# Retention samples: keys of each sample in a zero-padded matrix of 128 rows, and one sine table instead of two

## The chip, the cores and the metric

One core of a Trainium2 chip runs the whole program. The metric is device time in microseconds, as the median of several executions. Engines are named as in the profile: PE is TensorE (PEld its weight loads), DVE VectorE, ACT ScalarE, POOL GpSimd, SP SyncE, which issues the weight transfers.

## The reference, cut to what matters

One inference step of a two-layer decoder trunk for two groups of requests that share all weights: a prompt of 256 positions from zero state, and 8 samples of one position each from carried states. Layer 0 mixes with RWKV-7 and S5, layer 1 with retention, and a SwiGLU block follows each. Retention has 8 heads, with 256 query and key entries and 512 value entries each. For every sample and head the new state, a matrix of 256 x 512, is the old one times a decay plus an outer product, and the output is the query times the new state:

```
q = rotary(p[..., :D_MODEL]...);  k = rotary(...) * DK ** -0.5
S = S * chunk_decay + einsum('bjhd,bjhe->bhde', k, v)     # j = 1 for a sample
o = q S                                                  # what q reads of the new state
rotary(x): concatenate([x1 * cos - x2 * sin, x2 * cos + x1 * sin])
```

## The kernel before

Activations lie transposed: features on the 128 partitions, 264 columns (256 prompt positions, then 8 samples). All large weights stream through once. A *granule* is 4 blocks of 128x128 weights: SP loads them, ACT rounds them to the high part `wh`, DVE subtracts for the low part `wl`, and TensorE does three matmuls of 264 columns per block (`xh,wh`, `xh,wl`, `xl,wh`), 12 per granule. There are four buffers of each part, and `split_to` (line 467) runs two granules ahead of TensorE (`LS = 2`).

Everything else is *side work*: Python generators that record operations, which a planner places between the stream's matmuls. `pump` (line 516) is called twice per granule. It keeps a model clock for each engine, and emits a recorded operation when its operands are there by that clock; side matmuls are emitted only if `ready <= now`, with `now` the model clock of TensorE, and up to a budget. `cost` (line 213) holds the model's durations, `after` (line 240) its waits. It sees overlaps in cells of 16 columns (`GRAIN`), so neighbours that share a cell count as dependent. The order so planned is the order of each engine's queue on the chip, and each engine works its queue strictly in order; a waiting instruction holds up all that is behind it.

Buffers come from named areas. `hold` (line 359) takes a whole area (`hidx`, `hidy`, `hida`, `hidb`, `tmp`), `arenas` and `cut` (lines 417 and 422) slice small tiles from a list of areas, first fit. Layer 0 cuts its scratch from all five areas, `hidx` first; layer 1 cuts from `hidy` and `tmp` (`TMPN` = 14990 columns) and takes `hidx` (1056 columns) for the keys and values `kvr` of the samples.

In layer 1, `ret_mix(h)` (line 1475) does the prompt's part of head h, and `ret_sample(h)` (line 1555) the samples'. For each of the heads, `ret_sample`

- loads the states of samples 0 to 3, 512 KB each, through POOL's queue into `S`;
- spreads keys and values of the samples, split into a high and a low part, over zeroed matrices `kc` and `vc`, so that after a transpose the 8 rows 32b to 32b+7 hold sample 4g+b (high and low combinations, whose products add up);
- transposes the keys of all 8 samples (4 transposes into one PSUM bank) and copies them with one ACT instruction to `kr` (128x512); the same for the values, `vr`;
- for each group g of four samples and each sample b: two outer products with 8 rows and 512 columns, one for each half d of the keys, and behind each a DVE instruction that scales the old state and adds the product; then the store of the state:

```
rows = slice(32 * b, 32 * b + 8)
P.matmul(p, kr[rows, (2 * g + d) * 128:(2 * g + d + 1) * 128], vr[rows], start=True, stop=True)
self.stt(r["S"][b][:, d], r["S"][b][:, d], gam, p, OP.mult, OP.add)
```

- then multiplies the queries with the four states (8 matmuls with 32 output rows each), and after g = 0 loads the states of samples 4 to 7.

The rotation in `ret_mix` multiplies the two halves, swapped, with a table `ssin` that holds -sin and sin beside each other (528 columns; POOL), multiplies with `cos` in place and adds (DVE). The tables are loaded at the start of layer 1 by `ret_setup` (line 1441), which also clears `qm`, `kc` and `vc` on POOL.

Of the kernel before, what the change touches and what calls it, by code (L numbers as in the profile page):

```python
# [10 lines left out]
F32R = mybir.dt.float32r  # L11
I32 = mybir.dt.int32
AF = mybir.ActivationFunctionType
OP = mybir.AluOpType
# [6 lines left out]
T = TP + TS  # L21
# [11 lines left out]
HID = FFN_PARTS[1]  # L33
HIX = FFN_PARTS[0] - HID
RH, DK, DV = 8, 256, 512
TMPN = 14990
NSET = 2
MOST = 3.3, 2.6
GRAIN = 16
# [84 lines left out]
def bc(ap, shape):  # L124
    return ap.to_broadcast(shape)


class Builder:
# [287 lines left out]

    def arenas(self, names):

        size = {"hida": HID * T, "hidb": HID * T, "hidx": HIX * T, "hidy": HIX * T, "tmp": TMPN}
        self.ar = [[self.hold(n, [128, size[n]], F32, "ar_" + n), 0, size[n], n] for n in names]  # L420

    def cut(self, *shape, parts=128):
# [248 lines left out]
    def ffn_tasks(self, i):  # L671
        I = self.I
        wg, wu, wd = I["ffn_w_gate"][i], I["ffn_w_up"][i], I["ffn_w_down"][i]
        tasks = []
        st = {}
        sp = self.t1[:, KT * T:].rearrange("p (a t) -> p a t", a=8)
        f0 = 0
        for part, nf in enumerate(FFN_PARTS):
            def gate(acc, f):
                if f == 0 or f == FFN_PARTS[0]:  # L680
                    st["h"] = [self.hold("hida", [128, HID, T], F32R, "hh")]
                    st["l"] = [self.hold("hidb", [128, HID, T], F32R, "hl")]
                    if f == 0:
                        st["h"].append(self.hold("hidx", [128, HIX, T], F32R, "hhx"))
                        st["l"].append(self.hold("hidy", [128, HIX, T], F32R, "hly"))
                s = sp[:, f % 3]
                self.mul(s, acc[:, :T], self.rstd)
                self.act(s, s, AF.Silu)
                st[f] = s

            def up(acc, f, fl):
                u = sp[:, 3 + f % 2]
                self.mul(u, acc[:, :T], self.rstd)
                self.mul(u, u, st.pop(f))
                self.split(*rh(fl), u)

            def down(acc, k, part):
                if part and k == KT - 4:
                    self.functions(ACT_SET[AF.Ln])
                self.add(self.x[:, k], self.x[:, k], acc[:, :T])  # L700
                if part == len(FFN_PARTS) - 1:
                    self.x_final(i, k)

            rx = self.rx
            rh = lambda k: (st["h"][k // HID][:, k % HID], st["l"][k // HID][:, k % HID])
            for f in range(f0, f0 + nf, 2):
                for e in range(2):
                    tasks.append(Task(wg, 0, KT, (f + e) * 128, rx, lambda a, f=f + e: gate(a, f)))
                for e in range(2):
                    tasks.append(Task(wu, 0, KT, (f + e) * 128, rx, lambda a, f=f + e, fl=f + e - f0: up(a, f, fl)))  # L710
            for k in range(KT):
                tasks.append(Task(wd, f0, nf, k * 128, rh, lambda a, k=k, part=part: down(a, k, part)))
            f0 += nf
        return tasks
# [726 lines left out]
    def ret_setup(self):  # L1441
        self.arenas(["hidy", "tmp"])
        c = self.cut
        self.kvr = self.hold("hidx", [128, HIX * T], F32R, "kvr")
        self.omh = self.hold("hida", [128, HID, T], F32R, "omh")
        self.oml = self.hold("hidb", [128, HID, T], F32R, "oml")
        sp = self.t1[:, KT * T:]
        r = self.rm = dict(q=[c(2, T), c(2, T)], k=[c(2, T), c(2, T)], v=c(4, T), g=[c(4, T), c(4, T)], B=c(2, T), mask=c(TP),
                           att=c(TP + 128), vt=c(2, 512), kt=c(2, 256), S=[c(2, 512) for _ in range(4)],
                           kc=c(2, 2, 128), vc=c(4, 128), qm=c(2, TS, 32), st=c(2, 512),  # L1450
                           o=sp[:, :4 * T].rearrange("p (a t) -> p a t", a=4),
                           sq=sp[:, 4 * T:].rearrange("p (a t) -> p a t", a=4))
        o, n = CONST_AT["cos"][0], self.C0.shape[1]
        late = c(n - o)
        self.QS.dma_start(late, self.C0[:, o:])
        for name in ("cos", "ssin", "dist"):
            at, w = CONST_AT[name]
            self.k[name] = late[:, at - o:at - o + w]
        for n in ("qm", "kc", "vc"):
            self.G.memset(r[n], 0.0)  # L1460

    def ret_in(self, acc, n, h, i):
        r = self.rm
# [11 lines left out]
    def ret_mix(self, h):  # L1475
        r, k, P = self.rm, self.k, self.P
        B, o, sq = r["B"], r["o"], r["sq"]
        for n in "qk":
            yield from self.wait((n, h))
            x = r[n][h % 2]  # L1480
            self.tt(B, x[:, ::-1], k["ssin"].rearrange("p (a t) -> p a t", a=2), OP.mult, self.G)
            self.mul(x, x, bc(k["cos"][:, None, :], [128, 2, T]))
            self.add(x, x, B)
            yield
        self.flags.add(("rot", h))
        q, kk = r["q"][h % 2], r["k"][h % 2]
# [2 lines left out]
        p = self.psum()  # L1489
# [65 lines left out]
    def ret_sample(self, h):  # L1555

        r, k, P = self.rm, self.k, self.P
        yield from self.wait(("rs", h - 1))
        src, dst = self.I["state_ret"], self.O[7]

        def load(g):
            for b in range(4):
                self.QG.dma_start(r["S"][b], src[h, 4 * g + b])

        load(0)
        yield from self.wait(("rot", h), ("v", h))
        v, kk = r["v"][:, :, TP:], r["k"][h % 2][:, :, TP:]
        qm = r["qm"].rearrange("p a b c -> p a (b c)")[:, :, 0:7 * 33 + 1:33]
        self.gcopy(qm, r["q"][h % 2][:, :, TP:])

        for g in range(2):
            for x, to, hi, lo in ((kk, r["kc"][:, g], slice(0, 3, 2), slice(1, 4, 2)), (v, r["vc"], slice(0, 2), slice(2, 4))):
                n = to.shape[1]
                at = to.rearrange("p a (j w) -> p a j w", j=4)[:, :, :, 4 * g:4 * g + 4]
                x4 = bc(x[:, :, 4 * g:4 * g + 4, None], [128, n, 4, 2])
                self.act(at[:, :, :, hi].bitcast(F32R), x4, AF.Copy)
                self.tt(at[:, :, :, lo].bitcast(F32R), x4, at[:, :, :, hi], OP.subtract)
        self.flags.add(("kv", h))
        yield
        kr, vr = self.kvr[:, :512], self.kvr[:, 512:1024]  # L1580
        p = self.psum()
        for i in range(4):
            P.transpose(p[:, i * 128:(i + 1) * 128], r["kc"][:, i // 2, i % 2], self.ident)
        self.act(kr, p, AF.Copy)
        p = self.psum()
        for e in range(4):
            P.transpose(p[:, e * 128:(e + 1) * 128], r["vc"][:, e], self.ident)
        self.act(vr, p, AF.Copy)
        yield
        yield from self.wait(("ret", h - 1))  # L1590
        gam = math.exp(LOGG[h])
        po = self.banks[4]
        for g in range(2):
            for b in range(4):
                rows = slice(32 * b, 32 * b + 8)
                for d in range(2):
                    p = self.psum()
                    P.matmul(p, kr[rows, (2 * g + d) * 128:(2 * g + d + 1) * 128], vr[rows], start=True, stop=True)
                    self.stt(r["S"][b][:, d], r["S"][b][:, d], gam, p, OP.mult, OP.add)
                self.QG.dma_start(dst[h, 4 * g + b], r["S"][b])  # L1600
                yield
            for d in range(2):
                for b in range(4):
                    P.matmul(po[32 * b:32 * b + 32], r["qm"][:, d, 4 * g + b], r["S"][b][:, d],
                             start=g == 0 and d == 0, stop=g == 1 and d == 1, tile_position=(0, 32 * b))
            if g == 0:
                load(1)
            yield
        osb = self.flat(r["sq"])[:, :512]
        self.act(osb, po, AF.Copy)  # L1610
        yield
        p = self.psum()
        for e in range(4):
            P.matmul(p[:, 8 * e:8 * e + 8], osb[:, e * 128:(e + 1) * 128], k["sel"], start=True, stop=True)
        self.V.tensor_copy(r["o"][:, :, TP:], p[:, :32].rearrange("p (e b) -> p e b", e=4))
        self.flags.add(("rs", h))
        yield
# [71 lines left out]
def constants():  # L1689
# [4 lines left out]
    def put(name, a):  # L1694
        a = np.asarray(a, f)
        CONST_AT[name] = (sum(p.shape[1] for p in parts), a.shape[1])
        parts.append(a)
# [21 lines left out]
    pos = np.concatenate([np.arange(TP, dtype=f), np.full(TS, 2048.0, f)])  # L1719
    ang = (pos[None] * freq[:, None]).astype(f).astype(np.float64)  # L1720
    put("cos", np.cos(ang))
    put("ssin", np.concatenate([-np.sin(ang), np.sin(ang)], 1))
    tt = np.arange(TP)
    put("dist", np.where(tt[None] >= p[:, None], tt[None] - p[:, None], 1e6))
    return np.concatenate(parts, 1)
# [80 lines left out]
```

## Time and profile before

| | |
|---|---|
| median of 3 runs | 3178.41 us (3177.59 to 3178.79) |
| profiled execution | 3176.8 us, span 3174.9 us |
| mean granted clock of TensorE | 0.983 |
| busy: PE, DVE, ACT, POOL | 97%, 62%, 47%, 11% |
| HBM | 175 GB/s over the span |

The stretches of the program, by time from the start of the span: layer 0 to about 640 us, its SwiGLU block to about 1460, retention to about 2400 with the samples' outer products between 1535 and 2283, the second SwiGLU block to the end. Almost every instruction is recorded by one helper and carries line 279, so groups of instructions are told apart by their tiles. A matmul's record lasts longer than the time until the next may start, since matmuls overlap; what one adds to a chain is read from starts. The times of one kernel's runs lie within some 0.1% of each other here.

### The profile page before, as it was taken

The page shows a single profiled execution, that of the slowest core. Times are in us where ns is not written, and L with a number is a line of the kernel's source. Part 1 is how long each engine was busy: PE and PEld are TensorE (multiplying, and loading weights), DVE is VectorE, ACT ScalarE, POOL GpSimd, SP SyncE. Part 2 cuts the span into 40 slices and gives each one's busy share as a digit, 9 for nine tenths or more (in the row PEclk, how much of TensorE's full clock was granted, in tenths as well). Part 3 has the DMA queues.
Part 4 walks back from the last instruction along what each step waited for, and adds up shares of the span by engine and source line. Part 5 has one row for each costly group of instructions (what it writes and reads, how often), then busy time and mean ns, then how long its engine had stood idle before and what let it go on. Part 6 is the DMA issues. An engine that isn't in the chain of part 4 may idle for free.

```text
span 3174.9 us, 66100 instructions
## 1 busy us (share of the span) xinstructions
PE 3083.1 (97%) x26510; PEld 2941.5 (93%) x26510; DVE 1965.8 (62%) x3701; ACT 1498.3 (47%) x2734; POOL 341.6 (11%) x525
## 2 busy tenths in 40 slices
PE   7998898899999999999999999999999999999998
PEld 7987787799999999999889899998899999999998
DVE  6797676475555555556566666566566655556554
ACT  6543473255444444445434444444455444444454
POOL 5112332110000000001111111011100000000001
PEclk9999898799999999999999999999999999999999
DMA  5424324366665566656766667577666566666664
GB/s 195 121 89 96 51 80 79 67 184 182 180 182 184 180 181 179 185 180 207 240 227 230 222 229 261 159 264 241 220 182 183 180 185 181 181 182 180 183 181 152
DMA packets 161139, 560.56 MB, mean 177 GB/s; under 512 B 21312, under 2 KB 23744, under 8 KB 160576
## 3 DMA queue, kind: packets, MB, share of 16 engines
q1 hardware_dynamic: 140384, 483.29, 51.8%
q0 software_dynamic: 19584, 71.31, 6.0%
q8 instruction: 208, 3.41, 0.4%
q10 hardware_dynamic: 864, 1.74, 0.1%
q14 instruction: 99, 0.81, 0.1%
HBM read 511.45 MB, written 42.69 MB: 175 GB/s over the span
## 4 chain that ended last, share of the span: by engine, by line
PE 89%; DVE 4%; DMA 3%; ACT 2%; POOL 2%; issue 1%; SPq 0%; DVEq 0%; POOLq 0%; ACTq 0%
PE ps L279 89%; DMA ar_tmp<-ar_tmp 2%; DVE ar_tmp L279 2%; DVE wl L279 1%; DVE t L279 1%; ACT ar_tmp L279 1%; POOL ar_tmp L279 1%; ACT wh L279 0%; DVE ar_hida L279 0%; POOL sq L279 0%; DMA out_dram<-ar_tmp 0%; ACT t L279 0%; SPq L279 0%; POOL t L279 0%; POOL rstd L279 0%
## 5 line engine op out<-in xcount | busy, mean ns | idle before, releaser
L279 DVE TENSOR_TENSOR wl<-raw,wh 128x512 fp32r<-128x512 f32 x1784 | 1259.4, 710 | 901.1 <-ACT wh L279 889.3
L279 ACT ACTIVATE wh<-raw 128x512 fp32r<-128x512 f32 x1784 | 1099.7, 628 | 953.2 <-PE ps L279 916.3
L279 PE MATMUL ps<-xh,wh 128*128 128x264 f32 x4512 | 1326.3, 294 | 16.1 <-ACT wh L279 12.4
L279 PE MATMUL ps<-xh,wl 128*128 128x264 f32 x4512 | 1287.6, 285 | 10.1 <-DVE wl L279 10.0
L279 PE MATMUL ps<-xl,wh 128*128 128x264 f32 x4512 | 1284.8, 285 | 0.4 <-DVE xl L279 0.4
L279 PEld LDWEIGHTS ps<-xh,wh 128*128 128x128 f32 x4512 | 855.7, 190 | 64.3 <-issue 27.8
L279 PEld LDWEIGHTS ps<-xh,wl 128*128 128x128 f32 x4512 | 853.9, 189 | 12.3 <-DVE wl L279 12.3
L279 PEld LDWEIGHTS ps<-xl,wh 128*128 128x128 f32 x4512 | 856.8, 190 | 6.4 <-issue 5.1
L279 PE MATMUL ps<-hh,wl 128*128 128x264 f32 x1280 | 363.6, 284 | 0.0
L279 PE MATMUL ps<-hl,wh 128*128 128x264 f32 x1280 | 363.6, 284 | 0.0
L279 PE MATMUL ps<-hh,wh 128*128 128x264 f32 x1280 | 363.5, 284 | 0.0
L279 PE MATMUL ps<-n,wh 128*128 128x264 f32 x1408 | 257.4, 283 | 0.0
L279 PEld LDWEIGHTS ps<-hh,wh 128*128 128x128 f32 x1280 | 241.2, 188 | 0.0
L279 PEld LDWEIGHTS ps<-hl,wh 128*128 128x128 f32 x1280 | 240.7, 188 | 0.0
L279 PEld LDWEIGHTS ps<-hh,wl 128*128 128x128 f32 x1280 | 240.5, 188 | 0.0
L279 PE MATMUL ps<-ar_tmp 64*64 64x64 f32 (+8 forms) x2912 | 215.0, 282 | 18.6 <-DVE ar_tmp L279 9.2
L279 POOL TENSOR_TENSOR sqs<-sq,sqs 128x264 f32<-128x264 f32 x56 | 42.5, 760 | 1660.6 <-ACT sq L279 1660.6
L279 PEld LDWEIGHTS ps<-n,wh 128*128 128x128 f32 x1408 | 217.6, 188 | 0.0
L279 PEld LDWEIGHTS ps<-ar_tmp 64*64 64x64 f32 (+3 forms) x2912 | 148.4, 148 | 59.7 <-issue 22.8
L279 PE MATMUL ps<-n,wl 128*128 128x264 f32 x704 | 199.4, 283 | 0.0
L279 PE MATMUL ps<-omh,wh 128*128 128x264 f32 x512 | 146.9, 287 | 0.0
L279 PE MATMUL ps<-omh,wl 128*128 128x264 f32 x512 | 145.4, 284 | 0.0
(214 smaller groups left out, 2806.9 us busy)
## 6 DMA issues: line engine op xcount, KB each, us to landing
raw<-in_w_in_c_dram SPq DMA_DIRECT2D x192, 512.0 KB, 4.0
raw<-in_ffn_w_gate_dram SPq DMA_DIRECT2D x176, 512.0 KB, 3.7
raw<-in_ffn_w_up_dram SPq DMA_DIRECT2D x176, 512.0 KB, 3.6
raw<-in_ffn_w_down_dram SPq DMA_DIRECT2D x176, 512.0 KB, 3.6
out_dram<-ar_tmp POOLq DMA_DIRECT2D x72, 512.0 KB, 4.2
raw<-in_w_in_a_dram SPq DMA_DIRECT2D x68, 512.0 KB, 3.7
ar_tmp<-in_state_ret_dram POOLq DMA_DIRECT2D x64, 512.0 KB, 6.8
raw<-in_w_out_c_dram SPq DMA_DIRECT2D x64, 512.0 KB, 3.8
```

The lines of the kernel that those rows point to most:

```text
L279: getattr(eng.eng, name)(*a, **k)
```

## The change

The keys of a sample get a matrix of their own, `kr[j]`, 128 rows by 256 columns, which is zero outside the 8 rows of sample j of the group. The outer product then runs over all 128 rows of `kr[b]` and of the values. The four matrices hold one group of four samples at a time: `keys(g)` makes two transposes and four small copies, once ahead of the first group, and once more after the first group's queries. The rows outside are zeroed once, at the start of the layer, by copies of the zeroed `kc`. For the room, `hidx` grows from 1056 to 1536 columns and `tmp` shrinks by 480. The sine table is stored once; the rotation's product reads it twice, and the sign moves into a subtraction for the first half and an addition for the second.

```diff
-TMPN = 14990
+TMPN = 14510
+HIXN = 1536
@@ arenas
-        size = {"hida": HID * T, "hidb": HID * T, "hidx": HIX * T, "hidy": HIX * T, "tmp": TMPN}
+        size = {"hida": HID * T, "hidb": HID * T, "hidx": HIXN, "hidy": HIX * T, "tmp": TMPN}
@@ ret_setup
-        self.kvr = self.hold("hidx", [128, HIX * T], F32R, "kvr")
+        kr = self.hold("hidx", [128, HIXN], F32R, "kr")
+        self.kr = [kr[:, j * 256:(j + 1) * 256] for j in range(4)]
+        self.vr = kr[:, 1024:]
...
-        for name in ("cos", "ssin", "dist"):
+        for name in ("cos", "sin", "dist"):
...
         for n in ("qm", "kc", "vc"):
             self.G.memset(r[n], 0.0)
+        for j in range(4):
+            self.act(self.kr[j], self.flat(r["kc"])[:, :256], AF.Copy)
@@ ret_mix
-            self.tt(B, x[:, ::-1], k["ssin"].rearrange("p (a t) -> p a t", a=2), OP.mult, self.G)
+            self.tt(B, x[:, ::-1], bc(k["sin"][:, None, :], [128, 2, T]), OP.mult, self.G)
             self.mul(x, x, bc(k["cos"][:, None, :], [128, 2, T]))
-            self.add(x, x, B)
+            self.sub(x[:, 0], x[:, 0], B[:, 0])
+            self.add(x[:, 1], x[:, 1], B[:, 1])
@@ ret_sample
-        kr, vr = self.kvr[:, :512], self.kvr[:, 512:1024]
-        p = self.psum()
-        for i in range(4):
-            P.transpose(p[:, i * 128:(i + 1) * 128], r["kc"][:, i // 2, i % 2], self.ident)
-        self.act(kr, p, AF.Copy)
+        kr, vr = self.kr, self.vr
+
+        def keys(g):
+            p = self.psum()
+            for d in range(2):
+                P.transpose(p[:, d * 128:(d + 1) * 128], r["kc"][:, g, d], self.ident)
+            for j in range(4):
+                rows = slice(32 * j, 32 * j + 8)
+                self.act(kr[j][rows], p[rows, :256], AF.Copy)
+
+        keys(0)
...
-                rows = slice(32 * b, 32 * b + 8)
                 for d in range(2):
                     p = self.psum()
-                    P.matmul(p, kr[rows, (2 * g + d) * 128:(2 * g + d + 1) * 128], vr[rows], start=True, stop=True)
+                    P.matmul(p, kr[b][:, d * 128:(d + 1) * 128], vr, start=True, stop=True)
...
             if g == 0:
                 load(1)
+                keys(1)
```

## Rows read from the trace of the kernel before

**Rows 1.** The page, part 1: busy us (share of the span) and instructions.

```profile
PE 3083.1 (97%) x26510; PEld 2941.5 (93%) x26510; DVE 1965.8 (62%) x3701; ACT 1498.3 (47%) x2734; POOL 341.6 (11%) x525
```

**Rows 2.** Busy us by stretch: length, PE, PEld, DVE, ACT, POOL, clock, DMA, GB/s.

```profile
280.00:360.00 80.00, 61.59 (x642) 50.37 (x644) 58.44 (x143) 26.23 (x69) 32.35 (x48) 0.85 0.50 74
...
520.00:600.00 80.00, 57.00 (x648) 45.97 (x647) 33.12 (x70) 13.39 (x28) 13.65 (x12) 0.76 0.52 72
...
1520.00:2290.00 770.00, 770.00 (x5794) 694.26 (x5793) 470.36 (x786) 337.11 (x568) 112.03 (x167) 1.00 0.69 231
```

**Rows 3.** Groups, 1520 to 2290: count, busy us, mean ns, idle before.

```profile
L279 PE MATMUL ps<-xh,wh 128*128 128x264 f32 x1413 | 419.8, 297 | 0.0
...
L279 ACT ACTIVATE wh<-raw 128x512 fp32r<-128x512 f32 x410 | 254.2, 629 | 296.7 <-PE ps L279 289.2 <-DMA raw<-in_w_in_c_dram 2.1 <-DVE ar_tmp L279 1.9
...
L279 PE MATMUL ps<-kvr 8*128 8x512 f32 x128 | 46.7, 443 | 0.0
...
L279 DVE TENSOR_TENSOR ar_tmp<-ps,rstd 128x264 f32<-128x264 f32 x62 | 26.7, 431 | 15.3 <-PE ps L279 15.3
...
L279 DVE TENSOR_TENSOR ar_tmp<-ar_tmp 128x528 f32<-128x528 f32 x14 | 9.8, 697 | 1.2 <-POOL ar_tmp L279 1.2
...
L279 ACT ACTIVATE kvr<-ps 128x512 fp32r<-128x512 f32 x16 | 9.6, 599 | 35.5 <-PE ps L279 35.5
```

**Rows 4.** Busy us by stretch, columns as in rows 2: stream only.

```profile
2600.00:2700.00 100.00, 100.00 (x828) 100.00 (x827) 58.32 (x102) 47.16 (x83) 0.00 (x0) 1.00 0.61 182
```

**Rows 5.** Timeline of PE, first and last pair of products: start, us, instruction.

```profile
1535.39 0.28 PE L279 MATMUL ps<-xh,wl 128*128 128x264 f32 x1
1535.61 0.73 PE L279 MATMUL ps<-kvr 8*128 8x512 f32 x2
1536.27 0.39 PE L279 MATMUL ps<-xh,wh 128*128 128x264 f32 x1
1536.49 0.28 PE L279 MATMUL ps<-xl,wh 128*128 128x264 f32 x1
...
2282.20 0.28 PE L279 MATMUL ps<-omh,wl 128*128 128x264 f32 x1
2282.42 0.73 PE L279 MATMUL ps<-kvr 8*128 8x512 f32 x2
2283.07 0.40 PE L279 MATMUL ps<-omh,wh 128*128 128x264 f32 x1
2283.31 0.28 PE L279 MATMUL ps<-oml,wh 128*128 128x264 f32 x1
```

**Rows 6.** Timeline of PE around a group of four transposes.

```profile
1625.16 0.28 PE L279 MATMUL ps<-xh,wl 128*128 128x264 f32 x1
1625.28 0.60 PE L279 MATMUL ps<-cst,ar_tmp 128*128 128x128 f32 x4
1625.64 0.37 PE L279 MATMUL ps<-xh,wh 128*128 128x264 f32 x1
1625.84 0.28 PE L279 MATMUL ps<-xl,wh 128*128 128x264 f32 x1
```

**Rows 7.** Groups of the whole span, ScalarE copies of 256 columns.

```profile
L279 ACT ACTIVATE ar_tmp<-ar_tmp 128x256 f32<-128x256 f32 x24 | 9.8, 410 | 28.6 <-DVE ar_tmp L279 28.4
...
L279 ACT ACTIVATE ar_hidb<-ps 64x256 f32<-64x256 f32 x24 | 9.1, 378 | 13.1 <-PE ps L279 6.8 <-DVE ar_tmp L279 6.1
...
L279 ACT ACTIVATE ar_tmp<-ps 128x256 f32<-128x256 f32 x16 | 6.1, 378 | 58.8 <-PE ps L279 58.8
```

**Rows 8.** Waits, 1520 to 2290: us in total, times, longest.

```profile
ACT wh L279 <- PE ps L279: 289.2, 278, 2.9
```

**Rows 9.** The page, part 6: DMA issues, KB each, us to landing.

```profile
ar_tmp<-in_state_ret_dram POOLq DMA_DIRECT2D x64, 512.0 KB, 6.8
```

**Rows 10.** Timeline of POOL at the start of layer 1.

```profile
1462.39 2.35 POOL L279 DMA_DIRECT2D ar_tmp<-in_state_ret_dram  x4
1464.71 1.49 POOL L279 MEMSET ar_tmp<- 128x512 f32 x3
```

**Rows 11.** Waits of PE, 0 to 640: us in total, times, longest.

```profile
PE ps L279 <- DVE ar_tmp L279: 40.0, 20, 6.7
PE ps L279 <- ACT wh L279: 12.4, 2, 8.5
```

More of the change, by code (lines that the diff above doesn't have):

```diff
@@ L683, in gate @@
                     if f == 0:
-                        st["h"].append(self.hold("hidx", [128, HIX, T], F32R, "hhx"))
+                        st["h"].append(self.hold("hidx", [128, HIXN], F32R, "hhx")[:, :HIX * T].rearrange("p (a t) -> p a t", a=HIX))
                         st["l"].append(self.hold("hidy", [128, HIX, T], F32R, "hly"))
@@ L1721, in constants @@
     put("cos", np.cos(ang))
-    put("ssin", np.concatenate([-np.sin(ang), np.sin(ang)], 1))
+    put("sin", np.sin(ang))
     tt = np.arange(TP)
```

## The prediction

> **What bounds the kernel now.** I read the page's engine shares first: TensorE is busy for 97% of the span [rows 1]. That share is an average, so next come the stretches. The part of the program that the change is about runs from 1520 to 2290 us, where the retention samples do their work. TensorE is busy for all 770 us there, the granted clock is 1.00, VectorE works for 470 us, ScalarE for 337 and GpSimd for 112 [rows 2]. Busy alone says little of pipelined matmuls, so the third view is the groups of that stretch with the idle time before them: the stream's matmuls and the outer products both start with 0.0 us of idle before them [rows 3]. Nothing is waited for, so the length of this stretch is the sum of what each TensorE instruction takes from its predecessor's start to its own. A microsecond taken out of that sequence is a microsecond of the kernel, and work on the other engines is free until it makes TensorE wait.
>
> So the fourth view is the timeline of TensorE alone, read by starts. A stretch of stream only gives the pitch: 100 us hold 828 matmuls of 264 columns, 0.121 us each [rows 4]. Now the outer products. They stand in the stream as lone pairs, and the first and the last of them show the same picture [rows 5]. From the start of the last stream matmul before the pair to the start of the second one after it: 1536.49 - 1535.39 = 1.10 us and 2283.31 - 2282.20 = 1.11 us. Two stream matmuls lie in that, 0.24 us, so a pair costs 0.86 to 0.87 us. Starts are shown to 0.01 us, so I take 0.86. There are 128 outer products [rows 3], 8 heads by 8 samples by 2 halves, hence 64 pairs: 55 us. The reader is to see where a pair's time goes: the stream matmul ahead of it is given 0.22 us instead of 0.12, and the one behind it again 0.22. The kernel pays at the change of shape (8 rows against 128), not for columns alone.
>
> **The change part by part.**
>
> *Outer products over 128 rows.* The same 512 columns stream through, with the shape of the stream's own matmuls. No row shows a 512-column matmul of this kind, so I bound it by the stream's. At the upper of the clock's two levels, 2.4 GHz, its 264 columns at one a cycle are 0.110 us of the 0.121, and 0.011 is left over. For 512 columns that is 0.213 us if nothing is left over, 0.224 if the remainder belongs to the instruction, 0.235 if it grows with the columns. A pair then costs 0.43 to 0.47 us; I take 0.44, between the first two, since a longer run of columns gives more cover to whatever the remainder is. Saved per pair: 0.86 - 0.44 = 0.42 us; times 64, 26.9 us (from 0.39 x 64 = 25 to 0.43 x 64 = 27.5).
>
> The Trainium skill, page "TensorE: Matmul & The Clock Gate", section "Back-to-back issue gap", gives about 131 ns per matmul of 512 columns in a real stream; by it a pair is 0.26 us, the saving 38 us and the time 3140, an estimate from that page. The rows speak against it, since 264 columns alone already take 0.121 [rows 4].
>
> *Transposes of the keys in two groups of two.* Their number stays. Four of them cost 1625.84 - 1625.16 - 0.24 = 0.44 us, 0.11 each, with no visible cost of entering [rows 6]. One more group per head costs between nothing and the 0.08 us by which the stream's first matmul behind them is late: 0 to 0.7 us over 8 heads. I take 0.2.
>
> *Key copies.* Before: one 128x512 copy per head, 8 x 0.599 us [rows 3], since of the 16 copies there half are the values'. After: eight copies of 8x256 per head. The nearest rows read PSUM into 256 columns and take 0.378 us on 128 partitions and on 64 alike [rows 7], so fewer partitions are not cheaper: 64 x 0.378 = 24.2 us. ScalarE gains 24.2 - 4.8 = 19.4 us in 770, from 337 to 356: 46% busy. What hides them is the stream's lead. ScalarE's splits wait for TensorE 278 times in this stretch, 289 us in all [rows 8]: it is held back by free buffers, and could be earlier. If that cover were gone, four copies in a row, 1.5 us, would stand in front of a split.
>
> *The new wait in the middle of a head.* The second group's copies overwrite the first group's keys, so the second four samples wait for: last product of the first four, two transposes, four copies. Behind a waiting product on TensorE stands the whole stream. But products are placed in the program's order only when the planner's clock says that their operands are there, and stream matmuls fill the gap; the present copy of keys and values goes the same way, and the products behind it have 0.0 us of idle [rows 3]. Beside it runs the reload of the states for the same four samples, which takes longer than two transposes and four copies, 0.2 + 1.5 us: one load lands 6.8 us after its issue [rows 9]. I price it at nothing; the bound is in the rivals.
>
> *Rotation.* On VectorE one add of 128x528 (0.697 us) becomes a subtract and an add of 128x264. The nearest row of that width is 0.43 us [rows 3], so 16 x (0.86 - 0.70) = 2.6 us more, on an engine 61% busy. GpSimd's product keeps its 528 columns and only reads one table twice. Nothing on the path.
>
> *Zeroing, at the start of the layer.* Four ScalarE copies of 128x256, some 0.41 us each [rows 7], which wait for GpSimd to clear the padded keys. GpSimd clears three matrices in 1.49 us from 1464.71 on, after it has issued four loads [rows 10]; the planner doesn't count those issues. A split behind these copies may be up to some 3 us late (the 1.6 of the copies and the rest of the clearing), once, against a lead of two stream groups of 12 matmuls, 2.9 us. Cost 0 to 3 us; I take 0.3. The shorter table load moves 264 columns less; hidden.
>
> *Tile places.* One buffer grows by 480 columns, another shrinks by as much, and the first layer cuts its scratch from the same buffers by first fit. Walking through the list of cuts: the front's d, z, cum, t and P all move, neighbours that shared a 16-column cell (d with z, cum with t) no longer do, and others (the first hand's AR with BK) now do. The planner takes a shared cell for a dependence, so the first layer's instructions may come in another order. There TensorE does wait: between 280 and 360 us it is busy for 61.6 of 80, between 520 and 600 for 57.0 of 80, at granted clocks of 0.85 and 0.76 [rows 2], mostly behind VectorE [rows 11]. I see no direction in it: 0, with 8 us either way, about a fifth of the 41 us idle in these two stretches.
>
> **Sum.** 26.9 - 0.2 - 0.3 = 26.4 us off the path. The profiled execution took 3176.8 us (span 3174.9 and 1.9 around it), and gives 3150.4. The median of the runs shown is 3178.4, 1.6 above; for that I predict 3152. From its own terms (25 to 27.5 saved, 0 to 3.7 given back, 8 either way): 3178.4 - 27.5 - 8 = 3143 to 3178.4 - 25 + 3.7 + 8 = 3165; with a microsecond for the rounded starts, 3142 to 3165.
>
> **The rivals.**
>
> *The pair stays as dear.* Perhaps the time isn't in the change of shape but in each weight load that isn't hidden behind the matmul before it. Against it: the stream loads 128x128 weights before every matmul, and still keeps 0.121 us. For it: no row separates the load's part from the switch's. If all of it stayed, 3178 minus nothing: no change; if only the two outer boundaries went (0.1 us each of those seen in rows 5), 64 x 0.2 = 13 us and 3165. The Trainium skill, page "TensorE: Matmul & The Clock Gate", section "The mechanism" of its Part 3, holds that a weight load overlaps a running matmul only when its row group differs. By that rule full-height loads could never hide, and the change would save nothing. The stream's pitch in rows 4 does not bear it out.
>
> *Slower: TensorE stops for the second keys.* In each head, if the planner's clock runs ahead of ScalarE's, the first product of the second four samples reaches the head of TensorE's queue too early. Price, at its worst: the longest wait of a split, 2.9 us [rows 8], which ScalarE must pass first, one split of 0.63, and four copies of 0.378: 5.0 us, 8 heads, 40 us. 3178 - 26 + 40 = 3192. It decides from 3.3 us per head (26.4 / 8). Against it: no such stop in any of today's hand-overs.
>
> *The first layer loses its order.* If its waits grow by half of the 41 us, 3152 + 20 = 3172; if they shrink as much, 3132.
>
> **How the numbers follow.** The forecast, with its spread: 0.84. Pair stays dear: 0.03 fully, 0.05 half. First layer moved far: 0.03 worse, 0.02 better. TensorE stops: 0.03. A difference under 0.2%, 6.4 us, can't be told from none. Faster: 0.84 + 0.05 + 0.02 and a third of the worse order, 0.01, make 0.92; same: 0.03 + 0.01 = 0.04; slower: 0.03 + 0.01 = 0.04. The range 3142 to 3165 leaves out the pair fully dear, the far order both ways and the stop, 0.11, and some 0.04 of the forecast's own spread.
>
> **What would show it.** Right: a pair adds 0.43 to 0.47 us to the stream, the matmuls on both sides of it keep 0.12 us, the stretch of the samples is some 26 us shorter, and TensorE has no idle there. Wrong: idle in front of the fifth sample's product with ScalarE's key copy as releaser; products of 512 columns over 0.3 us apart; or a first layer whose end moved by more than 8 us.

## The result, and the profile after

The changed kernel takes 3158.92 us (median of 4 runs, 3158.68 to 3159.46) against 3178.26 us for the kernel before on the same chip: ratio 0.9941, 95% interval 0.9929 to 0.9952. That is 19.3 us faster, inside the range, with 7 us missing from the 26.4 that were expected. The profiled execution has a span of 3157.7 us, 17.2 us less than the one before.

What the change was for is seen in TensorE's timeline (start, length, instruction) of the changed kernel, at the first pair of products; it answers to [rows 5]:

```profile
1541.55 0.29 PE L280 MATMUL ps<-xh,wl 128*128 128x264 f32 x1
1541.67 0.63 PE L280 MATMUL ps<-kr 128*128 128x512 f32 x2
1542.14 0.28 PE L280 MATMUL ps<-xh,wh 128*128 128x264 f32 x1
1542.26 0.28 PE L280 MATMUL ps<-xl,wh 128*128 128x264 f32 x1
```

The matmuls around the pair now keep the stream's pitch of 0.12 us on both sides. From 1541.55 to 1542.26 are 0.71 us; less two stream matmuls that is 0.47 for the pair instead of 0.86. The groups of the stretch 1520 to 2290 us (count, busy us, mean ns, idle before), which answer to [rows 3]:

```profile
L280 PE MATMUL ps<-kr 128*128 128x512 f32 x128 | 40.1, 395 | 0.0
...
L280 ACT ACTIVATE kr<-ps 8x256 fp32r<-8x256 f32 x64 | 23.8, 372 | 25.5 <-PE ps L280 24.8
...
L280 DVE TENSOR_TENSOR ar_tmp<-ar_tmp 128x264 f32<-128x264 f32 x14 | 5.9, 424 | 0.0
```

The products still start with no idle before them. The small key copies take 0.372 us each, close to the 0.378 of the 64- and 128-partition rows of before, and the half-width halves of the rotation 0.424. Then the stretch of the samples (length, busy us of PE, PEld, DVE, ACT, POOL, clock, DMA, GB/s), which answers to [rows 2]:

```profile
1520.00:2290.00 770.00, 770.00 (x5998) 720.62 (x5997) 488.31 (x826) 371.19 (x649) 115.38 (x169) 1.00 0.70 236
```

In the same 770 us TensorE starts 5998 matmuls instead of 5794. Where the missing part went is read from milestones that both kernels share. The first load of a gate weight is issued when the mixing part of layer 0 is over, the first load of a weight of layer 1 when the SwiGLU block behind it is nearly over. Before (first and last start, us):

```profile
L279 SPq DMA_DIRECT2D raw<-in_ffn_w_gate_dram x176: 327/328/328, 691.2 to 3017.4; - x176
...
L279 SPq DMA_DIRECT2D raw<-in_w_in_c_dram x192: 327/328/328, 1461.2 to 2251.5; - x192
```

and after:

```profile
L280 SPq DMA_DIRECT2D raw<-in_ffn_w_gate_dram x176: 327/328/328, 700.8 to 3000.3; - x176
...
L280 SPq DMA_DIRECT2D raw<-in_w_in_c_dram x192: 327/328/328, 1469.1 to 2236.4; - x192
```

The gate weights start 9.6 us later than before and layer 1 7.9 us later; layer 1's last load of its weight is issued 15.1 us earlier, and the program ends 17.2 us earlier: from the start of layer 1 on the changed kernel gains 25.1 us. The expected gain was there, within its bounds (25 to 27.5), and some 8 us were lost before any retention work began.

### The profile page after: what moved, and what is told of

Read it like the earlier page. It is cut to its first block, busy times and chain, and to the rows that moved or that the text cites. A ratio compares the mean times of both kernels' runs of the same rounds, so it can differ in the third digit from the quotient of the medians.

```text
span 3157.7 us, 66191 instructions
## 1 busy us (share of the span) xinstructions
PE 3062.4 (97%) x26510; PEld 2947.8 (93%) x26510; DVE 1964.4 (62%) x3710; ACT 1516.0 (48%) x2801; POOL 345.7 (11%) x525
## 4 chain that ended last, share of the span: by engine, by line
PE 88%; DVE 5%; DMA 3%; ACT 1%; POOL 1%; issue 1%; SPq 0%; DVEq 0%; ACTq 0%; POOLq 0%
PE ps L280 88%; DMA ar_tmp<-ar_tmp 2%; DVE ar_tmp L280 2%; DVE wl L280 1%; DVE t L280 1%; POOL ar_tmp L280 1%; ACT ar_tmp L280 1%; ACT wh L280 0%; DVE ar_hidb L280 0%; POOL t L280 0%; DVE xl L280 0%; ACT t L280 0%; DVE ar_hida L280 0%; SPq L280 0%; POOL sq L280 0%
## 5 line engine op out<-in xcount | busy, mean ns | idle before, releaser
L280 PE MATMUL ps<-oml,wh 128*128 128x264 f32 x512 | 145.5, 284 | 0.0
```

The lines of the kernel that those rows point to most:

```text
L280: getattr(eng.eng, name)(*a, **k)
```

## The experiments

Two questions. Where do the 8 us of layer 0 come from: from the new places of its tiles (theory P), or was part of the gain lost in layer 1 (rival C)? And what was a pair of products paying for: the switch of shape (theory S) or the weight loads (rival W)?

**The change without its products.** The changed kernel, with the old products and key copy put back:

```diff
-        self.kr = [kr[:, j * 256:(j + 1) * 256] for j in range(4)]
-        self.vr = kr[:, 1024:]
+        self.kvr = kr
...
-        for j in range(4):
-            self.act(self.kr[j], self.flat(r["kc"])[:, :256], AF.Copy)
...
-                    P.matmul(p, kr[b][:, d * 128:(d + 1) * 128], vr, start=True, stop=True)
+                    P.matmul(p, kr[rows, (2 * g + d) * 128:(2 * g + d + 1) * 128], vr[rows], start=True, stop=True)
...
```

> The change without its outer products: new buffer sizes, one sine table, but the 8-row products and the one key copy per head of the kernel before. Theory P (the new places of the tiles reorder layer 0, which costs the 7.8 us by which layer 1 starts later): layer 1 starts near 1469 us as in the changed kernel, and the run is near 3186. Rival C (what is missing from the forecast is lost in layer 1, to key copies and zeroing): about 3178, layer 1 starting near 1461.

Measured 3184.97 us, before 3177.31: ratio 1.0026 (1.0016 to 1.0035). The start of layer 1 in its trace:

```profile
L280 SPq DMA_DIRECT2D raw<-in_w_in_c_dram x192: 327/328/328, 1472.1 to 2263.2; - x192
```

7.7 us are lost by the medians, with no new product and no new copy in the program. The nine runs of this kernel lie between 3183.15 and 3188.50 us, and the profiled one is the slowest of them: in it layer 1 starts 10.9 us late and the program ends 11.6 us late, so nearly all is lost before layer 1. Rival C falls.

**The change with layer 0's tiles in their old places.**

```diff
-        self.ar = [[self.hold(n, [128, size[n]], F32, "ar_" + n), 0, size[n], n] for n in names]
+        self.ar = [[self.hold(n, [128, size[n]], F32, "ar_" + n), 0, HIX * T if n == "hidx" else size[n], n] for n in names]
...
+        self.ar.insert(0, [self.ar[0][0], HIX * T, HIXN, "hidx+"])
         self.sv = {n: c(4, TS) for n in ("r", "k", "v", "kn", "b", "d", "rk", "y", "s1", "s2")}
```

> The changed kernel with layer 0's tiles at the places of the kernel before (the first 1056 columns of the grown buffer are cut as before; ten small sample vectors and two small matrices go to the new columns behind them). The order of layer 0 is then that of the kernel before. Theory P: layer 1 starts at 1461 or a little before it and the run is 3151 to 3153, 25 to 27 below the kernel before. Rival C: near 3159, no better than the changed kernel.

Measured 3149.71 us, ratio 0.9913 (0.9899 to 0.9928): 27.6 us faster than before, where the changed kernel was 19.3 us faster on its chip. Layer 1 starts where it did:

```profile
L280 SPq DMA_DIRECT2D raw<-in_w_in_c_dram x192: 327/328/328, 1461.1 to 2228.4; - x192
```

Up to that load the traces of this kernel and of the kernel before hold the same operations of the same shapes in the same order, on each of TensorE, VectorE, ScalarE and GpSimd. In the changed kernel VectorE's order departs at its 31st operation. The loss comes with the order that the new places bring, and this version beats both kernels. Not all of its 27.6 us are the products': from the start of layer 1 on it gains 25.1, like the changed kernel, and about 1.8 come from the SwiGLU block of layer 0 (last section).

**The sine table alone**, on the kernel before:

```diff
-            self.tt(B, x[:, ::-1], k["ssin"].rearrange("p (a t) -> p a t", a=2), OP.mult, self.G)
+            self.tt(B, x[:, ::-1], bc(k["sin"][:, None, :], [128, 2, T]), OP.mult, self.G)
...
-            self.add(x, x, B)
+            self.sub(x[:, 0], x[:, 0], B[:, 0])
+            self.add(x[:, 1], x[:, 1], B[:, 1])
```

> The kernel before with one sine table and the subtract and add of half the width, buffer sizes unchanged. All theories: 3178, within 1 us; VectorE busy 2 to 3 us longer in the stretch of the samples.

Measured 3178.58 us, ratio 1.0004 (0.9994 to 1.0013): nothing, as expected. The rotation's own VectorE instructions take 1.9 us more in the stretch of the samples (21.5 against 19.6), a little under the 2 to 3 expected; VectorE's busy time there is only 0.3 us longer in all.

**Every key copy twice**, on the changed kernel:

```diff
-                self.act(kr[j][rows], p[rows, :256], AF.Copy)
+                for _ in range(2):
+                    self.act(kr[j][rows], p[rows, :256], AF.Copy)
```

> The changed kernel with every small key copy issued twice: 64 more ScalarE copies, 24 us. Theory (the copies are hidden behind the stream's lead): 3159, within 2 us, no idle of TensorE in the stretch of the samples. Rival C (the copies cost what the forecast missed): 3159 + 7 = 3166 or more, with ScalarE as releaser of TensorE.

Measured 3158.33 us, against 3158.92 for the changed kernel. The groups of its stretch 1520 to 2290:

```profile
L280 ACT ACTIVATE kr<-ps 8x256 fp32r<-8x256 f32 x128 | 47.7, 373 | 27.0 <-PE ps L280 24.8
L280 PE MATMUL ps<-kr 128*128 128x512 f32 x128 | 40.2, 395 | 0.0
```

24 us more of ScalarE's time change nothing. The new wait in the middle of a head, which these copies end, has cover to spare.

**Two samples side by side**, on the kernel before (8 rows each, so that the two products of a pair lie in different row groups; the stores move behind both samples):

```diff
-            for b in range(4):
-                for d in range(2):
+            for b0 in (0, 2):
+                for d in range(2):
+                    for b in (b0, b0 + 1):
...
```

> The kernel before with its 8-row products in another order: two samples side by side, so that the two products of a pair lie in different groups of rows (b and b+1, same half d). Theory S (the cost is the switch between 8 and 128 rows, at the two ends of a pair): a pair still costs 0.86 us and the run is 3178. Theory W (each weight load that shares rows with the matmul ahead of it is exposed by 0.10 to 0.12 us, the middle one too): the middle one is hidden, a pair costs 0.74 us or less, the run is 3170 or lower. If the two products even run beside each other, a pair costs some 0.5 us and the run is near 3155.

Measured 3162.11 us, ratio 0.9952 (0.9935 to 0.9968). Its timeline of TensorE shows two kinds of island (products in a row between two stream matmuls), 8 of four products and 48 of two:

```profile
1534.17 0.28 PE L279 MATMUL ps<-xh,wl 128*128 128x264 f32 x1
1534.38 0.73 PE L279 MATMUL ps<-kvr 8*128 8x512 f32 x4
1535.04 0.39 PE L279 MATMUL ps<-xh,wh 128*128 128x264 f32 x1
1535.27 0.29 PE L279 MATMUL ps<-xl,wh 128*128 128x264 f32 x1
...
1559.46 0.28 PE L279 MATMUL ps<-xh,wl 128*128 128x264 f32 x1
1559.67 0.50 PE L279 MATMUL ps<-kvr 8*128 8x512 f32 x2
1560.11 0.39 PE L279 MATMUL ps<-xh,wh 128*128 128x264 f32 x1
1560.34 0.28 PE L279 MATMUL ps<-xl,wh 128*128 128x264 f32 x1
```

Two products in different row groups cost 1560.34 - 1559.46 - 0.24 = 0.64 us, where two in the same one cost 0.86. Four, which are two such pairs in sequence, cost 1.10 - 0.24 = 0.86. So the row groups do run beside each other, one round of 512 columns for both, and a second round adds 0.22 us, its columns. Its weight loads lie on the same rows as the round before and cost nothing to be seen. By the figures on record the run fell on W's side (0.74 us or less and 3170 or lower, against 0.86 and 3178), and what came true of them is their last sentence, the products beside each other. W falls by the islands of four, and by a single product in a later run, which costs 0.62 us: the second product of a pair in one row group adds 0.24, its 512 columns, and no exposed load. Theory S stands in so far as the rest is paid once per island; it had not said that rounds would be shared.

What the switch consists of is not separated by any run. The weight loads (PEld) of the kernel before at the pair of [rows 5]:

```profile
1535.61 0.29 PEld L279 LDWEIGHTS ps<-kvr 8*128 8x128 f32 x2
...
1536.27 0.19 PEld L279 LDWEIGHTS ps<-xh,wh 128*128 128x128 f32 x1 [0.37 <-issue]
```

and of the changed kernel at its first pair:

```profile
1541.55 0.31 PEld L280 LDWEIGHTS ps<-kr 128*128 128x128 f32 x2
...
1541.91 0.19 PEld L280 LDWEIGHTS ps<-xh,wh 128*128 128x128 f32 x1
```

In the changed kernel a load starts one matmul ahead of its own, at 1541.55 for the product at 1541.67. Before, at both ends of the pair, it starts only together with its own matmul, at 1535.61 and at 1536.27. So the loads at the two ends, though not the one within the pair, may be part of what the switch costs.

**32 rows instead of 128**, the changed kernel with one thing undone:

```diff
-                    P.matmul(p, kr[b][:, d * 128:(d + 1) * 128], vr, start=True, stop=True)
+                    P.matmul(p, kr[b][32 * b:32 * b + 32, d * 128:(d + 1) * 128], vr[32 * b:32 * b + 32], start=True, stop=True)
```

> The changed kernel with one thing undone: its products read only the 32 rows of their own row group of the padded keys and values (8 rows filled, 24 zero), everything else, order included, as changed. Theory S (the cost is the switch between the stream's 128-row shape and a row group): a pair costs 0.86 us again, 64 x (0.86 - 0.465) = 25 us come back, near 3184, with layer 0 as in the changed kernel. Rival (it is the 8 rows themselves that are slow, too few for the array): a pair near 0.47 and the run near 3159.

Measured 3181.7 us, 22.8 above the changed kernel (ratio to before 1.0012, 1.0003 to 1.0022). Its timeline:

```profile
1541.04 0.28 PE L280 MATMUL ps<-xh,wl 128*128 128x264 f32 x1
1541.25 0.73 PE L280 MATMUL ps<-kr 32*128 32x512 f32 x2
1541.91 0.39 PE L280 MATMUL ps<-xh,wh 128*128 128x264 f32 x1
1542.14 0.28 PE L280 MATMUL ps<-xl,wh 128*128 128x264 f32 x1
```

1.10 us again, as in [rows 5]. All 64 pairs together cost 54.8 us, as before the change. A product that reads all 32 rows of its row group pays what 8 rows paid; of the heights that were run, only the full one is free of it.

**Four samples side by side**, on the kernel before, to use what the pairs had shown (the stores move behind all eight products of a group):

```diff
-            for b in range(4):
-                for d in range(2):
+            for d in range(2):
+                for b in range(4):
...
```

> The kernel before, 8-row products, but for each half of the keys the products of four samples side by side, one in each group of 32 rows: 32 islands of four. From the run with two samples side by side: 0.40 us per island for the switch and 0.23 for each round of 512 columns, however many row groups take part. Theory S (switch at the two ends, row groups run beside each other): 32 x 0.63 = 20 us instead of 55, 35 us less, near 3143, and better than 128 rows at 64 x 0.465 = 30 us. Rival (only two products fit beside each other): 32 x 0.86 = 27.4, 27 us less, near 3150. Rival W (each of the four loads is exposed by 0.1): 32 x 1.03 = 33 us, near 3156.

A miss: 3188.16 us, ratio 1.0031 (1.0019 to 1.0042), slower than before. Its timeline of TensorE:

```profile
1537.91 0.51 PE L279 MATMUL ps<-kvr 8*128 8x512 f32 x4
1538.35 0.39 PE L279 MATMUL ps<-xh,wh 128*128 128x264 f32 x1
...
1540.01 2.07 PE L279 MATMUL ps<-kvr 8*128 8x512 f32 x4
1542.01 0.39 PE L279 MATMUL ps<-xh,wh 128*128 128x264 f32 x1
```

and VectorE's:

```profile
1538.44 0.69 DVE L279 SCALAR_TENSOR_TENSOR ar_tmp<-ar_tmp,ps 128x512 f32<-128x512 f32 x1 [1.77 <-PE ps L279]
1539.05 0.68 DVE L279 TENSOR_TENSOR wl<-raw,wh 128x512 fp32r<-128x512 f32 x1
1539.65 2.47 DVE L279 SCALAR_TENSOR_TENSOR ar_tmp<-ar_tmp,ps 128x512 f32<-128x512 f32 x4
```

The first island is as cheap as expected: 0.44 us from its start to the stream. It fills all four shared PSUM banks. The next four products are in the queue 2.1 us later, before VectorE has drained them; they get the banks one by one as it does, and hold the stream for 2 us. Of the 32 islands 16 cost 0.63 us and 16 about 2.2. The second island reaches TensorE while three of the four banks are still to be drained; why the planner's model has it there so early is not shown. The planner books 0.60 us for a drain whose record lasts 0.69, but in the trace one drain starts 0.6 us after the other, so the booking alone does not explain it. This is the kind of stop that I had priced as a rival for the second keys, at another hand-over.

The stops are not the whole loss. Behind seven of the 16 the granted clock falls to its lower level, the first time at 1542.9 us (length, busy us, clock, DMA and GB/s as in [rows 2]):

```profile
1543.00:1546.00 3.00, 3.00 (x15) 3.00 (x15) 2.72 (x5) 0.63 (x1) 1.60 (x3) 0.50 0.84 274
```

Fifteen matmuls start in these 3 us, where the stream's pitch would give 25. All such stretches between 1540 and 2202 us last 24 us together, and at half the pace some 12 us are lost in them. Against the forecast the stops themselves cost 25 us, six waits of 1.2 us of the stream's own matmuls for VectorE another 7, and layer 1 starts 2.3 us late.

**The same, with the drain booked at 0.95 us:**

```diff
+            if name == "scalar_tensor_tensor" and n == 512:
+                return 0.95
```

> Four row groups side by side as in the run before, but the planner books 0.95 us instead of 0.60 for the VectorE instruction that drains a product's bank, so that the next four come later. They now stand in 40 islands (24 of four, 8 of three and 8 single ones). Theory (the run with four row groups lost its gain because the next four products waited for VectorE to drain the four shared banks): no such waits, 40 x 0.63 = 25 us instead of 55, near 3148. Rival (VectorE falls behind whatever the spacing, and the stream's own splits wait): 3170 or more, with TensorE waiting for VectorE.

Measured 3159.58 us, ratio 0.9943 (0.993 to 0.9955), 11 us above the 3148 expected and below the rival's 3170: the 2-us stops are gone, but not all waits, and the clock stays at 1.00. Eight of the 24 islands of four still cost 1.3 to 1.8 us instead of 0.64. What is left of TensorE's waits between 640 and 2300 us (us in total, times, longest):

```profile
PE ps L281 <- DVE ar_tmp L281: 4.3, 7, 0.7
PE ps L281 <- DVE t L281: 2.8, 2, 1.5
```

In its timeline stand an island of four and one of a single product:

```profile
1535.73 0.28 PE L281 MATMUL ps<-xh,wl 128*128 128x264 f32 x1
1535.95 0.51 PE L281 MATMUL ps<-kvr 8*128 8x512 f32 x4
1536.39 0.39 PE L281 MATMUL ps<-xh,wh 128*128 128x264 f32 x1
1536.61 0.29 PE L281 MATMUL ps<-xl,wh 128*128 128x264 f32 x1
...
1540.76 0.28 PE L281 MATMUL ps<-xh,wl 128*128 128x264 f32 x1
1540.97 0.49 PE L281 MATMUL ps<-kvr 8*128 8x512 f32 x1
1541.39 0.39 PE L281 MATMUL ps<-xh,wh 128*128 128x264 f32 x1
1541.62 0.28 PE L281 MATMUL ps<-xl,wh 128*128 128x264 f32 x1
```

One product costs 0.62 us, four in different row groups 0.64. With the pair of [rows 5] at 0.86 this gives the price list here: about 0.40 us for going to a row group's shape and back, and 0.23 for each round of 512 columns. It also shows the limit of the changed kernel's way: four products cost 2 x 0.47 = 0.94 us at full height and 0.64 in four row groups. I didn't find an order in which those 0.3 us aren't lost to VectorE.

**Which shared cells?** First the kernel before with planner cells of one column, so that no neighbours count as dependent:

```diff
-GRAIN = 16
+GRAIN = 1
```

> The kernel before, planner cells of 1 column instead of 16, so that no two tiles count as dependent because they share a cell. Read against its partner with the change. Its own time may go either way by up to 10 us, since layer 0 gets a third order.

Measured 3178.96 us, ratio 1.0007 (0.9997 to 1.0016). Then the changed kernel with the same edit:

> The changed kernel with planner cells of 1 column. Theory P (the new places act through shared cells alone): layer 0 has the order of its partner, layer 1 starts within 2 us of it, and the whole run is 24 to 27 us faster than the partner. Rival A (the places themselves, the addresses, cost time): layer 1 starts some 8 us later than in the partner and the run is only 17 to 20 us faster.

Measured 3149.65 us, ratio 0.9909 (0.9895 to 0.9922): 29.3 us below its partner, 2 more than expected; the partner's ten runs spread from 3176.67 to 3186.72, so the 2 us say nothing. The starts of layer 1, partner's first:

```profile
L279 SPq DMA_DIRECT2D raw<-in_w_in_c_dram x192: 327/328/328, 1462.6 to 2252.7; - x192
```

```profile
L280 SPq DMA_DIRECT2D raw<-in_w_in_c_dram x192: 327/328/328, 1458.8 to 2226.2; - x192
```

With the same new places, but no shared cells, layer 0 loses nothing. The two traces hold the same order of operations up to these loads, on all four engines, so the 3.8 us by which layer 1 starts earlier, where 2 were expected at most, lie within what one order varies by here. The places act through the planner's cells, and no cost of the addresses is to be seen.

Then an attempt to name the cells: the changed kernel with tiles of the third area moved up, so that AR, BK, P and the mixed outputs share none.

```diff
         self.omm = c(26)
+        self.ar[2][1] += -self.ar[2][1] % 16
-        self.fs = dict(d=c(TP), z=c(2, T), cum=c(TP), t=c(TP), P=c(NC_, C + 1), w=c(128))
+        self.fs = dict(d=c(TP), z=c(2, T), cum=c(TP), t=c(TP), P=c(NC_, C + 1))
+        self.ar[2][1] += -self.ar[2][1] % 16
+        self.fs["w"] = c(128)
```

> The changed kernel with the tiles that layer 0 cuts from the third area (hida) moved up to the next multiple of 16 columns in two places (10 and 12 columns are skipped), so that AR and BK of the first hand, P and the mixed outputs share no planner cell with a neighbour any more. Theory P2 (those shared cells are what costs layer 0 its time): layer 1 starts near 1461 and the run is near 3150. Rival (any new place gives another order, and the order's cost has no such direction): layer 1 starts anywhere between 1459 and 1472, most likely not within 2 us of 1461.

Measured 3162.14 us, ratio 0.995 (0.9934 to 0.9967), and

```profile
L280 SPq DMA_DIRECT2D raw<-in_w_in_c_dram x192: 327/328/328, 1471.7 to 2239.1; - x192
```

a late layer 1 again. It was not these cells, or not these alone; another order came out, at least as dear as the changed kernel's. What in the order costs the 8 us stays open. Part of it can be read: over the first 710 us TensorE is busy 627.4 us after and was 630.4 before, and the granted clock is 0.92 instead of 0.93. The changed kernel:

```profile
0.00:710.00 710.00, 627.41 (x6781) 563.55 (x6782) 498.43 (x1232) 334.46 (x716) 187.03 (x299) 0.92 0.41 104
```

the kernel before:

```profile
0.00:710.00 710.00, 630.41 (x6855) 565.65 (x6856) 509.04 (x1251) 340.08 (x723) 185.25 (x301) 0.93 0.42 106
```

So about 3 us are waits, and the rest goes with a slightly lower clock in a stage where TensorE stops and starts. These are single executions: without the new products TensorE was busy for 629.0 us at 0.92 with a greater loss, so the shares move from run to run.

## Why the prediction was right, and where it was off

*Outer products: right in kind, a little off in size.* I took 0.44 us per pair; summed over the starts around all 64 pairs, less the pitch of the stream matmuls between them, the trace has 29.9 us, 0.465 each, where it had 54.8. That is close to my upper bound, columns at the stream's own pitch: 0.235 for 512, against 0.233 measured. The choice of 0.22 took the remainder of the stream's pitch for a fixed cost of an instruction, or less; most of it grows with the columns. That is 64 x 0.025 = 1.6 us of the sum. The other figure that the prediction names, 0.26 us for a pair, did not come.

*Transposes, key copies, the wait in the head, zeroing, rotation: right.* From the start of layer 1 the gain is 25.1 us; 64 x 0.39 is 25, so these edits together cost nothing that shows. Doubling the copies and the table alone say the same, and VectorE's 2.6 us for 16 rotations came out as 1.9 for the 14 that lie in the stretch. The stop for the second keys did not come.

*Tile places: the step that failed.* "I see no direction in it: 0, with 8 us either way" became +7.9 us at the start of layer 1 in the profiled run, +7.7 with the products taken out, and -27.6 instead of -19.3 when the old places were kept. The mechanism, shared cells that change the order, was the one I had named; the value was a coin's toss, and fell on the dear side. The bound held only by luck. At the end of layer 0's mixing part the loss was 9.6 us, over the bound and over the 8 us that the prediction names as a sign of being wrong; some 1.8 us that the SwiGLU block gained, and that the prediction had not foreseen, brought it under 8. So the time came out inside the range with one term of the sum wrong by its whole bound. The profile held nothing that gave its sign. What could have been seen: any edit of a buffer size that a first-fit shares with another stage changes that stage too, and can be fenced off.

*The rule on weight loads.* I weighed the Trainium skill's rule that a load overlaps a running matmul only if its row group differs (page "TensorE: Matmul & The Clock Gate", section "The mechanism" of its Part 3). The same section of the Trainium skill also lets a load run ahead that goes to a background weight buffer, which my reading left out. The second round of an island of four reloads rows that the first round is using and adds 0.22 us, no more than its columns, so no run here bears the rule out. The same section of the Trainium skill shows matmuls in different row groups running beside each other; here one product costs 0.62 us and four 0.64, which agrees. I had passed that by, because the kernel before never had two row groups next to each other. And the Trainium skill, page "TensorEngine Tiling (Array Packing)", section "Key Properties", says that a change of tiling mode drains TensorE: the 0.40 us per island may be that, or the late weight loads at the two ends, or both, and no run here tells them apart. The 32-row run shows that they come with the shape and not with the number of rows read, 8 or 32.

## What to carry to other kernels

A few small matmuls with fewer rows, alone in a stream of full-height ones, paid here for the change of shape at both ends; padding their operands with zeros to the full height made them ordinary, with the zeros made once. When an edit resizes a shared buffer, keep the other stages' tiles where they were, or time the resize by itself: here it took back 8 of some 27 us. And before many row groups are put side by side, ask who drains the banks, and what a stop of TensorE does to its clock.

## What the runs showed that I had not expected

Four products in four row groups take 0.64 us, one takes 0.62: on TensorE the work of the other three is free, and only the drain of their results isn't. In the SwiGLU block of layer 0 all seven kernels with the new buffer sizes gain another 1.7 to 2.1 us between the first gate weights and layer 1 (from 9.6 us late to 7.9 in the changed kernel), and none with the old sizes does; its cause is open.
